# The order of SP's loads between the end of the attention and the output projection of a hybrid encoder block

## The chip, the cores and the metric

One core of a Trainium2 chip runs the whole block in one launch. The metric is device time in microseconds (us). Three runs of the kernel before gave a median of 1238.97 us (1238.19 to 1239.67). One more execution was profiled; all rows below come from it.

## What is computed

The reference, cut to the parts that this case touches. All arrays are float32; the sequence is 1024 tokens plus 16 meta tokens, the model width is 1024, and the MLP is 4096 wide.

```python
def hybrid_mixer(u, ...):
    z = jnp.einsum('bld,dn->bln', u, w_in)
    a, q, k, v, r, lr, ga, gb = jnp.split(z, IN_SPLITS, axis=-1)
    ...
    y_a = jnp.einsum('blc,cd->bld', p, w_pool_out)
    ...
    o = gla_chunked(q, k, v, log_a)
    o = rmsnorm(o, gla_norm...) * jax.nn.silu(r)...
    y_b = jnp.einsum('blc,cd->bld', o.reshape(B, L, GLA_VAL), w_gla_out)
    m = jax.nn.sigmoid(ga) * y_a + jax.nn.sigmoid(gb) * y_b
    return jnp.einsum('bld,de->ble', m, w_out)

def reference(x, ...):
    ...
    h = h + hybrid_mixer(rmsnorm(h, norm_mix[l]), ...)
    h = h + squared_relu_mlp(rmsnorm(h, norm_ffn[l]), w_ff1[l], w_ff2[l])
    return rmsnorm(h, norm_final)[:, N_META:]
```

## The kernel before

Every float32 product is made of three passes over rounded operands: each operand is split into a high part (`hi`, written by ACT with a copy that rounds) and a low part (`lo`, the remainder, written by DVE or POOL with a subtraction), and `mm3` (lines 246 to 248) issues high by high, high by low and low by high into one PSUM bank. A weight therefore takes three steps before PE may use it: SP's DMA brings it into a raw tile, ACT makes the high part, DVE (or POOL) makes the low part.

The work is a list of steps that runs once in the order of the program. PE keeps that order. Two regions have a hand-made order on other engines too: `in_order(True)` in `early_gates` starts a stretch in which ACT and DVE are kept in program order, and `wo1_open` ends it. Everywhere else, and on SP and POOL in the whole kernel, a scheduler sets the order when the program is built. Each engine, SP's queue included, works through its list in order: an instruction that waits holds back all that stand behind it.

The stretch of this case, in the order of the program:

- **The last attention unit** closes: `across` (from line 1216) normalizes the result and writes the high and low parts of `yg` (lines 1280 and 1281). PE fills its waits with blocks of the product with `w_gla_out`.
- **The gates.** `yb_block(n, h)` multiplies `yg` by a 256-column block of `w_gla_out`, two output tiles of 128 by 512 for each block, for the token half h. Each of the eight output tiles of a half is called a gate here, G0 to G7 in half 0 and H0 to H7 in half 1. A gate takes 12 matmuls, two loads (`gl` from `gb_dram`, line 1008, and `ml` from `ma_dram`, line 1009), two DVE operations (line 1060 takes the product out of PSUM and multiplies it by `gl`, line 1061 adds `ml`), an ACT operation (`th`, line 1064) and a POOL operation (`tl`, line 1065). The tiles for the loads rotate over three places in each half, so the loads of a gate wait for the DVE and POOL operations of the gate three back.
- **The blocks' weights** go through the ring `W1` (class `Ring`, lines 58 to 80): raw load at line 101, high part at line 77, low part at line 78. Half 1 uses the blocks 2, 3, 0, 1: the blocks 2 and 3 are kept from half 0, and blocks 0 (gates H4, H5) and 1 (gates H6, H7) are loaded again.
- **The output weights.** `load_wo(ch, kk)` loads 256 rows of one column half of `w_out` (512 KB) into a raw tile (line 101), makes the high part on ACT (line 1345) and the low part on DVE (line 1346). The four pieces of the first column half are called kk0 to kk3. They share the two raw tiles, and a third one (`raw3`), with the ring's loads: `raw.lend(S["raw3"])` in `merge_open`.
- **x again.** `x_again(t)` (line 1337) loads the t-th tile of 128 rows of x (512 KB) into `acc[:, t]`, since the residual is added there.
- **The output projection.** `out_tile(t, ch)` multiplies rows tile t of the merged gates by column half ch of `w_out`, 24 matmuls, and DVE adds the bank into `acc` (line 1378). The eight tiles of ch 0 run first; tile 0 needs kk0 to kk3 one after the other, 6 matmuls each. After ch 1 the rows are normalized and turned for the MLP.

Four PSUM banks rotate over the gates of half 1 and the tiles of the projection, so a gate or tile needs the bank of the fourth one before it to have been taken out by DVE.

Of the kernel before, what the change touches and what calls it, by code (L numbers as in the profile page):

```python
# [15 lines left out]
P = 128  # L16
D = 1024
# [3 lines left out]
HALF = 512  # L21
# [15 lines left out]
class Stack:  # L37


    def __init__(self, tc, side):  # L40
        self.tc, self.side, self.pools = tc, side, []
# [17 lines left out]
class Ring:  # L59


    def __init__(self, nc, raw, hi, lo, depth):
        self.nc, self.raw, self.hi, self.lo, self.depth = nc, raw, hi, lo, depth
        self.queue, self.loaded, self.done, self.kept = [], 0, 0, 0
        self.views = {}
        self.eng = nc.vector

    def top_up(self):
        while self.loaded < min(self.done + self.depth, len(self.queue)):
            ap = self.queue[self.loaded]  # L70
            s = self.loaded % self.depth
            n = 1
            for k in ap.shape[1:]:
                n *= k
            raw = self.raw.load(ap, n)
            hi, lo = self.hi[:, s, :n], self.lo[:, s, :n]
            self.nc.scalar.activation(hi, raw, ACT.Copy)
            self.eng.tensor_tensor(lo, raw, hi.bitcast(F32), ALU.subtract)
            self.views[self.loaded] = (hi, lo)
            self.loaded += 1  # L80
# [25 lines left out]
def kernel(  # L106
# [3 lines left out]
    nc = tc.nc  # L110
# [3 lines left out]
    w_gate_up, b_gate, gla_norm, w_gla_out, w_out = w_gate_up[0], b_gate[0], gla_norm[0], w_gla_out[0], w_out[0]  # L114
# [65 lines left out]
    raw = Raw(nc, [left.push(f"raw{i}", [P, D], F32) for i in range(2)])  # L180
    W1 = Ring(nc, raw, left.push("w1h", [P, 2, D], F32R), left.push("w1l", [P, 2, D], F32R), 2)
# [9 lines left out]
    def f32(ap):  # L191
        return ap.bitcast(F32)
# [4 lines left out]
    def bcast(v):  # L197
        return v[None, :].broadcast_to([P, D])
# [599 lines left out]
    one = []  # L798
# [122 lines left out]
    def rows4(w, j):  # L921
        return w[:, j * 256 : (j + 1) * 256].rearrange("(k p) c -> p k c", p=P)
# [79 lines left out]
    def yb_load(n, h):  # L1002

        if n >= 8 or (n, h) in staged:
            return
        d = 2 * YB[h][n // 2] + n % 2
        gl, ml = staged[n, h] = (nxt("t2"), nxt("o2")) if h else (nxt("t1"), nxt("o"))
        nc.sync.dma_start(gl, gb_dram[d, h])
        nc.sync.dma_start(ml, ma_dram[d, h])

    def in_order(on):


        if on:
            S["order"] = tc.manual_schedule(engines={mybir.EngineType.Activation, mybir.EngineType.DVE})
            S["order"].__enter__()
        else:
            S.pop("order").__exit__(None, None, None)

    def early_gates():  # L1020

        in_order(True)
        left.pop_to(S["left_n"])
        for key in ("t2", "o2"):
            S[key] = right.push(key, [P, 3, HALF], F32)
            S["n" + key], S["d" + key] = 0, 3
        S["raw3"] = right.push("raw3", [P, D], F32)
        for n in range(3):
            yb_load(n, 1)

# [294 lines left out]
    def merge_open():  # L1325
        W1.eng = dve
        banks(keep=1, x=2, ms=4)
        rota["mm"] = ("mm", "mm", "x", "x")
        left.pop_to(base)
        S["wo"] = [left.push("wo0", [P, 2, KT, HALF], F32R)]  # L1330
        S["left_acc"] = left.mark()
        S["acc"] = left.push("acc", [P, 8, D], F32)
        raw.lend(S["raw3"])
        nc.sync.dma_start(gB, bcast(norm_ffn))

    def x_again(t):
        nc.sync.dma_start(S["acc"][:, t], x[t * P : (t + 1) * P, :])

    def load_wo(ch, kk):
        def fn():  # L1340
            wo = S["wo"][ch][:, :, 2 * kk : 2 * kk + 2]
            c = slice(ch * HALF, (ch + 1) * HALF)
            r = raw.load(w_out[kk * 256 : (kk + 1) * 256, c].rearrange("(k p) c -> p k c", p=P), D)
            r = r.rearrange("p (k c) -> p k c", k=2)
            act.activation(wo[:, 0], r, ACT.Copy)
            dve.tensor_tensor(wo[:, 1], r, f32(wo[:, 0]), ALU.subtract)

        return fn

    step(one, merge_open)  # L1350
    def wo1_open():
        in_order(False)
        raw.back()
        right.pop_to(0)
        buffer("u2", 2, D)
        S["u2p"] = right.push("u2p", [P, 2, HALF], F32)
        S["rawx0"] = right.push("rawx0", [P, D], F32)
        raw.lend(S["rawx0"])
        S["right_ff"] = right.mark()
        S["wo"].append(right.push("wo1", [P, 2, KT, HALF], F32R))  # L1360
# [54 lines left out]
            dve.tensor_tensor(fl, a, f32(fh), ALU.subtract)  # L1415

    for n, j in enumerate(YB[1]):
        if n < 2:
            step(one, yb_block(n, 1))
        else:  # L1420
            step(one, yb_block(n, 1), W1, [rows4(w_gla_out, j)])
        if n:
            step(one, load_wo(0, n - 1))
    step(one, load_wo(0, 3))
    step(one, wo1_open)
    for t in range(8):
# [12 lines left out]
    for t in ORDER[:6]:  # L1439
        step(one, out_tile(t, 1))  # L1440
# [258 lines left out]
```

## Time and profile before

| what | value |
|---|---|
| median of 3 runs | 1238.97 us (1238.19 to 1239.67) |
| the profiled execution | 1239.98 us |
| its span, first to last instruction | 1238.2 us |
| PE busy in the span | 1207.4 us (98%) |
| DVE, ACT, POOL busy | 852.3, 618.3, 66.3 us |
| mean granted clock of PE | 0.995 |
| PE busy from 500 to 600 us | 93.90 of 100 us, clock 0.97 |

The profiled execution's time is 1.78 us above its span; that is the time around the first and the last instruction. Changes inside the span are added to or taken from the median. In a timeline row the columns are start in us, duration in us, engine, line, operation, the tile written and the tile read, and the count; in brackets stands the idle time ahead of it on its engine and what ended that.

### The profile page before, as it was taken

To read this page: it belongs to the slowest core of one execution; us is meant where nothing else is said; L and a number is where in the kernel's file an instruction comes from. 1 tells how busy PE (TensorE), PEld (TensorE's weight loads), DVE (VectorE), ACT (ScalarE), POOL (GpSimd) and SP (SyncE) were. 2 spreads that over 40 slices of the span, in tenths; PEclk is the share of its full clock that TensorE was granted. 3 is DMA by queue.
4 is the path that set the end of the run, shared out by engine and by line. 5 is a ranking of instruction groups with operands and counts; after the bars stand their busy time and mean duration, and the time that the engine had idled before them with its cause. 6 is when DMAs were issued, how large, how long until landed. Compare 5 with 4: busy or idle time off the path is not lost.

```text
span 1238.2 us, 18288 instructions
## 1 busy us (share of the span) xinstructions
PE 1207.4 (98%) x6816; PEld 1006.6 (81%) x6816; DVE 852.3 (69%) x1388; ACT 618.3 (50%) x1099; POOL 66.3 (5%) x74
## 2 busy tenths in 40 slices
PE   7999999999999999899999999999999999999997
PEld 6978888888897778688878888888888888888886
DVE  5896676564456686633897776766775877887686
ACT  6677667322446664412664554545554444444554
POOL 2100000001101115400000000000000000000000
PEclk9999999999999999999999999999999999999999
DMA  8033326247102237741144444444559983333532
GB/s 250 2 96 117 111 85 186 61 139 235 35 19 78 69 120 247 264 127 51 70 137 152 164 155 141 158 149 162 162 198 322 342 268 102 94 97 100 162 97 90
DMA packets 142680, 173.84 MB, mean 140 GB/s; under 512 B 10968, under 2 KB 82416, under 8 KB 142592
## 3 DMA queue, kind: packets, MB, share of 16 engines
q1 hardware_dynamic: 142592, 172.68, 43.7%
q8 instruction: 53, 0.87, 0.3%
q14 instruction: 35, 0.29, 0.1%
HBM read 119.17 MB, written 53.48 MB: 139 GB/s over the span
## 4 chain that ended last, share of the span: by engine, by line
PE 87%; DVE 7%; ACT 3%; issue 1%; DMA 1%; SPq 0%; DVEq 0%; ACTq 0%
PE b_mm L246 10%; PE b_mm L247 10%; PE b_mm L248 10%; PE b_ms L248 9%; PE b_ms L246 9%; PE b_ms L247 9%; PE b_x L247 8%; PE b_x L246 8%; PE b_x L248 8%; PE b_sc L1147 1%; PE b_ms L550 1%; PE b_mx L246 1%; PE b_m L1249 1%; PE b_mx L248 1%; PE b_mx L247 1%
## 5 line engine op out<-in xcount | busy, mean ns | idle before, releaser
L246 PE MATMUL b_mm<-th,w1h 128*128 128x512 f32 (+1 forms) x312 | 117.7, 377 | 0.6 <-ACT th L1406 0.6
L247 PE MATMUL b_mm<-tl,w1h 128*128 128x512 f32 (+1 forms) x312 | 116.2, 372 | 0.6 <-DVE tl L1407 0.6
L248 PE MATMUL b_mm<-th,w1l 128*128 128x512 f32 (+1 forms) x312 | 116.0, 372 | 0.0
L246 PE MATMUL b_x<-th,w1h 128*128 128x512 f32 (+1 forms) x240 | 90.8, 378 | 0.0
L247 PE MATMUL b_x<-tl,w1h 128*128 128x512 f32 (+1 forms) x240 | 90.7, 378 | 0.0
L248 PE MATMUL b_x<-th,w1l 128*128 128x512 f32 (+1 forms) x240 | 90.4, 377 | 0.0
L264 ACT ACTIVATE w1h<-raw 128x512 fp32r<-128x512 f32 x96 | 59.5, 620 | 34.7 <-PE b_x L247 14.1
L265 DVE TENSOR_TENSOR w1l<-raw,w1h 128x512 fp32r<-128x512 f32 x96 | 65.7, 685 | 10.9 <-ACT w1h L264 10.9
L264 ACT ACTIVATE w1h<-fs 128x512 fp32r<-128x512 f32 x72 | 45.4, 630 | 46.2 <-PE b_ms L247 31.8
L246 PEld LDWEIGHTS b_mm<-th,w1h 128*128 128x128 f32 x312 | 58.6, 188 | 12.0 <-ACT th L1406 1.0
L247 PEld LDWEIGHTS b_mm<-tl,w1h 128*128 128x128 f32 x312 | 58.7, 188 | 10.6 <-DVE tl L1407 0.9
L248 PEld LDWEIGHTS b_mm<-th,w1l 128*128 128x128 f32 x312 | 58.7, 188 | 10.3
L264 ACT ACTIVATE w1h<-bt 128x512 fp32r<-128x512 f32 x44 | 27.8, 632 | 67.9 <-issue 63.6
L265 DVE TENSOR_TENSOR w1l<-fs,w1h 128x512 fp32r<-128x512 f32 x72 | 49.3, 686 | 14.7 <-ACT w1h L264 14.6
L1556 DVE TENSOR_TENSOR bt<-w,w 128x512 f32<-128x512 f32 x80 | 54.7, 684 | 1.1 <-DMA w<-in_w_ff_dram 1.1
L248 PEld LDWEIGHTS b_x<-th,w1l 128*128 128x128 f32 x240 | 45.2, 188 | 8.4
L246 PEld LDWEIGHTS b_x<-th,w1h 128*128 128x128 f32 x240 | 45.1, 188 | 8.4
L247 PEld LDWEIGHTS b_x<-tl,w1h 128*128 128x128 f32 x240 | 45.1, 188 | 8.2
L264 ACT ACTIVATE fxh<-bt 128x512 fp32r<-128x512 f32 x36 | 22.8, 632 | 54.9 <-issue 49.2
L247 PE MATMUL b_ms<-wo,w1h 128*128 128x512 f32 x128 | 49.8, 389 | 0.0
L248 PE MATMUL b_ms<-wo,w1l 128*128 128x512 f32 x128 | 49.8, 389 | 0.0
L246 PE MATMUL b_ms<-wo,w1h 128*128 128x512 f32 x128 | 49.8, 389 | 0.0
(446 smaller groups left out, 3373.9 us busy)
## 6 DMA issues: line engine op xcount, KB each, us to landing
hf_dram<-h SPq DMA_DIRECT2D x112, 256.0 KB, 2.1
raw<-hf_dram SPq DMA_DIRECT2D x112, 256.0 KB, 2.7
w<-in_w_ff_dram SPq DMA_DIRECT2D x64, 256.0 KB, 4.7
raw<-in_w_in_dram SPq DMA_DIRECT2D x24, 512.0 KB, 4.8
raw<-in_w_ff_dram SPq DMA_DIRECT2D x16, 512.0 KB, 4.1
rawx<-in_w_ff_dram SPq DMA_DIRECT2D x16, 512.0 KB, 4.2
xs<-in_x_dram SPq DMA_DIRECT2D x8, 512.0 KB, 4.6
rawx<-in_w_in_dram SPq DMA_DIRECT2D x8, 512.0 KB, 4.6
```

The source lines that it names most:

```text
L246: pe.matmul(ps, ah, bh, start=first and i == 0, stop=False, skip_group_check=more)
L247: pe.matmul(ps, ah, bl, start=False, stop=False, skip_group_check=more)
L248: pe.matmul(ps, al, bh, start=False, stop=last and i == n - 1, skip_group_check=more)
L264: act.activation(hi, a, ACT.Copy)
L265: dve.tensor_tensor(lo, a, f32(hi), ALU.subtract)
L550: pe.transpose(b[j][:, i], u[:, (4 * j + i) * P : (4 * j + i + 1) * P], ident)
L1147: pe.matmul(b[to, e, j], kk[r, s], qq[r, s], start=True, stop=True, tile_position=(e * CH, u * CH))
L1249: pe.matmul(o[part(u), e, j], scc[part(u), e, j], v[part(u), j, e], start=j == 0, stop=False, tile_position=(u * CH, u * CH), skip_group_c ...
L1556: dve.tensor_tensor(bt, w, S["w2"][q[3:]][:, i], ALU.add if q[2] == "+" else ALU.subtract)
```

## The change

- `Ring` gets a `fetch` that issues raw loads ahead of the conversions, and `top_up` uses what was fetched.
- `merge_open` closes the ordered stretch of ACT and DVE and opens it again, and from there to `first_blocks` SP's loads stand in program order too (`in_order("loads", ...)`).
- The third raw tile is no longer lent to the ring. It takes kk0, issued in `early_gates` ahead of the gates of half 1. kk1, kk2 and kk3 are loaded into `acc[:, 5]`, `acc[:, 6]` and `acc[:, 7]`, which hold nothing yet at that time.
- `load_wo(0, n)` moves ahead of the block n of half 1, where it stood behind the block n + 1.
- The x loads, and the load of the norm's weights (`gB`), move behind the last gate's loads; x then runs two tiles ahead of the projection.
- No arithmetic is added or removed.

```diff
+    def fetch(self, count):
+
+        for ap in self.queue[self.loaded + len(self.fetched) :][:count]:
             n = 1
             for k in ap.shape[1:]:
                 n *= k
-            raw = self.raw.load(ap, n)
+            self.fetched.append((self.raw.load(ap, n), n))
+
+    def top_up(self):
+        while self.loaded < min(self.done + self.depth, len(self.queue)):
+            s = self.loaded % self.depth
+            if not self.fetched:
+                self.fetch(1)
+            raw, n = self.fetched.pop(0)
...
     def early_gates():
...
         S["raw3"] = right.push("raw3", [P, D], F32)
+        fetch_wo(0, 0, S["raw3"])
         for n in range(3):
             yb_load(n, 1)
...
         S["acc"] = left.push("acc", [P, 8, D], F32)
-        raw.lend(S["raw3"])
+        any_order("order")
+        in_order("loads", mybir.EngineType.SP)
+        in_order("order", mybir.EngineType.Activation, mybir.EngineType.DVE)
+        W1.fetch(2)
+        fetch_wo(0, 1, S["acc"][:, 5])
+
+    def load_gB():
         nc.sync.dma_start(gB, bcast(norm_ffn))
...
     for n, j in enumerate(YB[1]):
+        step(one, load_wo(0, n))
         if n < 2:
             step(one, yb_block(n, 1))
         else:
             step(one, yb_block(n, 1), W1, [rows4(w_gla_out, j)])
-        if n:
-            step(one, load_wo(0, n - 1))
-    step(one, load_wo(0, 3))
+        if n < 2:
+            step(one, lambda kk=n + 2: fetch_wo(0, kk, S["acc"][:, 4 + kk]))
+    step(one, load_gB)
     step(one, wo1_open)
+    step(one, lambda: x_again(0))
+    step(one, lambda: x_again(1))
     for t in range(8):
-        step(one, lambda t=t: x_again(t))
+        if t < 6:
+            step(one, lambda t=t: x_again(t + 2))
         step(one, out_tile(t, 0))
         if 1 < t < 6:
             step(one, load_wo(1, t - 2))
...
     def first_blocks():
+        any_order("loads")
```

PE's and POOL's instructions keep their order. What moves on the other engines, as the built programs have it, at the three places that matter:

**Place 1, the gate G3 in the attention's close.** ACT, from the gates G1 and G2 (`th_131` is half 0's high part, `w1h` the ring's) to the first operations of the last normalization, before:

```order
L1064 ACTIVATE th_131<-t_2709 128x512 x2
L77 ACTIVATE w1h<-raw_115 128x1024
L1064 ACTIVATE th_131<-t_2709 128x512
L1268 ACTIVATE mix<-b_m_4639 128x1024
L210 ACTIVATE small<-small 128x8
L212 ACTIVATE small<-small 128x8
```

and of the change:

```order
L1071 ACTIVATE th_131<-t_2709 128x512 x2
L1369 ACTIVATE wo_4805<-raw_4539 128x1024
L83 ACTIVATE w1h<-raw_115 128x1024
L1071 ACTIVATE th_131<-t_2709 128x512
L1275 ACTIVATE mix<-b_m_4640 128x1024
L216 ACTIVATE small<-small 128x8
L218 ACTIVATE small<-small 128x8
```

DVE at the same place, from gate G2's sum to the reduction that starts the normalization, before:

```order
L1061 TENSOR_TENSOR t_2709<-t_2709,o 128x512
L1254 COPY small<-b_m_4639 128x2
L1060 TENSOR_TENSOR t_2709<-b_mm,t_2709 128x512
L1061 TENSOR_TENSOR t_2709<-t_2709,o 128x512
L1271 TENSOR_REDUCE small<-mix 128x8
L211 TENSOR_SCALAR small<-small 128x8
```

and of the change:

```order
L1068 TENSOR_TENSOR t_2709<-t_2709,o 128x512
L1261 COPY small<-b_m_4640 128x2
L1067 TENSOR_TENSOR t_2709<-b_mm,t_2709 128x512
L1370 TENSOR_TENSOR wo_4805<-raw_4539,wo_4805 128x1024
L1068 TENSOR_TENSOR t_2709<-t_2709,o 128x512
L1278 TENSOR_REDUCE small<-mix 128x8
L217 TENSOR_SCALAR small<-small 128x8
```

The high part of kk0 stands ahead of the ring's weight and of G3's `th` on ACT, and its low part stands between the two operations of G3 on DVE.

**Place 2, the gates of half 1.** ACT, from the last gates of half 0 over the ring's two weights to the last gates (`th_139` is half 1's), before:

```order
L1064 ACTIVATE th_139<-t_4531 128x512
L77 ACTIVATE w1h<-raw_119 128x1024
L1064 ACTIVATE th_139<-t_4531 128x512 x2
L77 ACTIVATE w1h<-raw_4539 128x1024
L1064 ACTIVATE th_139<-t_4531 128x512
L1345 ACTIVATE wo_4804<-raw_115 128x1024
L1064 ACTIVATE th_139<-t_4531 128x512 x2
L1345 ACTIVATE wo_4804<-raw_119 128x1024
L1064 ACTIVATE th_139<-t_4531 128x512 x2
L1345 ACTIVATE wo_4804<-raw_4539 128x1024
L1345 ACTIVATE wo_4804<-raw_115 128x1024
```

and of the change:

```order
L1071 ACTIVATE th_139<-t_4531 128x512
L83 ACTIVATE w1h<-raw_119 128x1024
L1071 ACTIVATE th_139<-t_4531 128x512
L1369 ACTIVATE wo_4805<-acc 128x1024
L1071 ACTIVATE th_139<-t_4531 128x512
L83 ACTIVATE w1h<-raw_115 128x1024
L1071 ACTIVATE th_139<-t_4531 128x512
L1369 ACTIVATE wo_4805<-acc 128x1024
L1071 ACTIVATE th_139<-t_4531 128x512 x2
L1369 ACTIVATE wo_4805<-acc 128x1024
L1071 ACTIVATE th_139<-t_4531 128x512 x2
```

Before, kk0, kk1 and the pair kk2 and kk3 followed H3, H5 and H7; now kk1 stands between H1 and H2, ahead of the ring's second weight, kk2 behind H3 and kk3 behind H5. The low parts on DVE moved in the same way: kk1's stands behind H1's sum and ahead of H2, kk3's behind H5 and ahead of H6.

**Place 3, SP's queue over half 1** (`t_4531` and `o_4535` are the gates' loads of half 1), before, from G7's load on:

```order
L1008 DMA t_2709<-gb_dram 128x512
L1337 DMA acc<-in_x_dram 128x1024
L1008 DMA t_4531<-gb_dram 128x512
L1009 DMA o_4535<-ma_dram 128x512
L1337 DMA acc<-in_x_dram 128x1024
L101 DMA raw_119<-in_w_out_dram 128x2x512
L1008 DMA t_4531<-gb_dram 128x512
L1009 DMA o_4535<-ma_dram 128x512
L1008 DMA t_4531<-gb_dram 128x512
L1009 DMA o_4535<-ma_dram 128x512
L101 DMA raw_4539<-in_w_out_dram 128x2x512
L1009 DMA o_4535<-ma_dram 128x512
```

and of the change, from kk1 to the last gate's load:

```order
L1361 DMA acc<-in_w_out_dram 128x2x512
L1014 DMA t_4531<-gb_dram 128x512
L1015 DMA o_4535<-ma_dram 128x512
L1361 DMA acc<-in_w_out_dram 128x2x512
L1014 DMA t_4531<-gb_dram 128x512
L1015 DMA o_4535<-ma_dram 128x512
L1014 DMA t_4531<-gb_dram 128x512
L1015 DMA o_4535<-ma_dram 128x512
L1361 DMA acc<-in_w_out_dram 128x2x512
L1014 DMA t_4531<-gb_dram 128x512
L1015 DMA o_4535<-ma_dram 128x512
L1014 DMA t_4531<-gb_dram 128x512
```

kk1 took the place of the first x load, the x loads left the stretch, and all four pieces of the first column half are issued ahead of the loads of H6.

More of the change, by code (lines that the diff above doesn't have):

```diff
@@ L63, in __init__ @@
         self.nc, self.raw, self.hi, self.lo, self.depth = nc, raw, hi, lo, depth
-        self.queue, self.loaded, self.done, self.kept = [], 0, 0, 0
+        self.queue, self.loaded, self.done, self.kept, self.fetched = [], 0, 0, 0, []
         self.views = {}
         self.eng = nc.vector
[L68 to L71, printed above, removed]
+    def fetch(self, count):
+        for ap in self.queue[self.loaded + len(self.fetched) :][:count]:
             n = 1
@@ L1009, in yb_load, with in_order, any_order @@
         nc.sync.dma_start(ml, ma_dram[d, h])
[L1011 to L1018, printed above, removed]
+    def in_order(key, *engines):
+        S[key] = tc.manual_schedule(engines=set(engines))
+        S[key].__enter__()
+    def any_order(key):
+        S.pop(key).__exit__(None, None, None)
     def early_gates():
-        in_order(True)
+        in_order("order", mybir.EngineType.Activation, mybir.EngineType.DVE)
         left.pop_to(S["left_n"])
@@ L1332, in merge_open @@
         S["acc"] = left.push("acc", [P, 8, D], F32)
-        raw.lend(S["raw3"])
+        any_order("order")
+        in_order("loads", mybir.EngineType.SP)
+        in_order("order", mybir.EngineType.Activation, mybir.EngineType.DVE)
+        W1.fetch(2)
+        fetch_wo(0, 1, S["acc"][:, 5])
+    def load_gB():
         nc.sync.dma_start(gB, bcast(norm_ffn))
@@ L1337, in x_again, with fetch_wo @@
         nc.sync.dma_start(S["acc"][:, t], x[t * P : (t + 1) * P, :])
+    fetched = {}
+    def fetch_wo(ch, kk, at=None):
+        c, rows = slice(ch * HALF, (ch + 1) * HALF), w_out[kk * 256 : (kk + 1) * 256]
+        ap = rows[:, c].rearrange("(k p) c -> p k c", p=P)
+        if at is None:
+            at = raw.load(ap, D)
+        else:
+            nc.sync.dma_start(at.rearrange("p (k c) -> p k c", k=2), ap)
+        fetched[ch, kk] = at.rearrange("p (k c) -> p k c", k=2)
     def load_wo(ch, kk):
         def fn():
[L1341 to L1344, printed above, removed]
+            if (ch, kk) not in fetched:
+                fetch_wo(ch, kk)
+            wo, r = S["wo"][ch][:, :, 2 * kk : 2 * kk + 2], fetched.pop((ch, kk))
             act.activation(wo[:, 0], r, ACT.Copy)
@@ L1351, in wo1_open @@
     def wo1_open():
-        in_order(False)
+        any_order("order")
         raw.back()
```

## The prediction

> **What bounds the kernel now.** The page has PE busy for 98% of the span, so only PE's idle time can be won. The list of PE's waits shows most of it at one place (waiter, line, releaser: us in all, times, longest):
>
> ```profile
> PE b_mm L246 <- ACT wo L1345: 4.1, 1, 4.1
> PE b_mm L247 <- DVE wo L1346: 2.0, 2, 1.4
> ```
>
> Both are tile 0 of the output projection, waiting for the high and low parts of w_out. PE's timeline, from gate H6 to the second tile:
>
> ```profile
> 509.54 0.39 PE L246 MATMUL b_x<-yg,w1h 128*128 128x512 f32 x1
> ...
> 514.98 0.39 PE L246 MATMUL b_mm<-wo,th 128*128 128x512 f32 x1
> ...
> 518.29 0.50 PE L247 MATMUL b_mm<-wo,th 128*128 128x512 f32 x1 [1.36 <-DVE wo L1346]
> ...
> 523.78 0.80 PE L246 MATMUL b_mm<-wo,th 128*128 128x512 f32 x1 [4.05 <-ACT wo L1345]
> ...
> 529.44 0.39 PE L246 MATMUL b_x<-wo,th 128*128 128x512 f32 x1
> ```
>
> H6 and H7, 24 matmuls, took 514.98 - 509.54 = 5.44 us (0.227 each). Tile 0, also 24, took 529.44 - 514.98 = 14.46. So 9.02 us are lost, of which 6.1 are waits; the rest is a halved clock after them (windows: start and end, length, busy us of PE, PEld, DVE, ACT and POOL, PEclk, DMA share, GB/s):
>
> ```profile
> 521.00:522.00 1.00, 0.00 (x0) 0.00 (x0) 0.97 (x2) 0.00 (x0) 0.57 (x1) 0.90 0.78 215
> 522.00:528.00 6.00, 3.53 (x8) 2.47 (x9) 4.36 (x5) 4.64 (x5) 1.27 (x1) 0.50 0.85 320
> 528.00:529.00 1.00, 1.00 (x5) 0.83 (x4) 0.62 (x1) 0.00 (x0) 0.00 (x0) 0.69 0.96 324
> ```
>
> Why the weights came late, on ACT, DVE and SP:
>
> ```profile
> 522.15 0.63 ACT L1064 ACTIVATE th<-t 128x512 fp32r<-128x512 f32 x1 [1.92 <-DVE t L1061]
> 522.69 1.99 ACT L1345 ACTIVATE wo<-raw 128x1024 fp32r<-128x1024 f32 x2
> 520.50 0.69 DVE L1060 TENSOR_TENSOR t<-b_mm,t 128x512 f32<-128x512 f32 x1 [0.94 <-DMA t<-gb_dram]
> 512.13 0.38 SPq L101 DMA_DIRECT2D raw<-in_w_out_dram  x1
> 515.94 0.33 SPq L1008 DMA_DIRECT2D t<-gb_dram  x1
> ```
>
> kk2 and kk3 (the pair at 522.69) stand on ACT behind the last gate H7, whose load left SP only at 515.94. Tile 0 needs half 0 alone, so H7 need not have held it.
>
> **The change, part by part.** *Removed: the 9.02 us.* kk2 and kk3 now stand ahead of H7, with their loads ahead of H6's. If no new wait arises, the gain is 9.0, its upper end. The four copies and four subtractions are paid for all the same, now inside the gates.
>
> *kk0 inside G3.* The rows of G2 and G3 on ACT and DVE, the end of the attention's chain, a low part of w_out beside POOL, and the two PE instructions that need the chain:
>
> ```profile
> 479.15 0.63 ACT L1064 ACTIVATE th<-t 128x512 fp32r<-128x512 f32 x1 [1.92 <-DVE t L1061]
> 480.36 0.69 DVE L1060 TENSOR_TENSOR t<-b_mm,t 128x512 f32<-128x512 f32 x1 [0.73 <-PE b_mm L248]
> 481.08 0.69 DVE L1061 TENSOR_TENSOR t<-t,o 128x512 f32<-128x512 f32 x1
> 481.81 0.63 ACT L1064 ACTIVATE th<-t 128x512 fp32r<-128x512 f32 x1 [0.58 <-DVE t L1061]
> 482.35 1.01 ACT L1268 ACTIVATE mix<-b_m 128x1024 f32<-128x1024 f32 x1
> 486.30 1.23 DVE L1273 TENSOR_TENSOR mix<-b_m,small 128x1024 f32<-128x1024 f32 x1
> 492.44 1.23 DVE L1281 TENSOR_TENSOR yg<-mix,yg 128x1024 fp32r<-128x1024 f32 x1 [1.13 <-ACT yg L1280]
> 510.64 1.47 DVE L1346 TENSOR_TENSOR wo<-raw,wo 128x1024 fp32r<-128x1024 f32 x1 [1.65 <-ACT wo L1345]
> 488.92 1.03 PE L1277 MATMUL b_m<-ident,mix 128*128 128x128 f32 x8
> 494.81 0.39 PE L247 MATMUL b_mm<-yg,w1h 128*128 128x512 f32 x1
> ```
>
> ACT's copy fits behind G2's th (479.7 to 480.75). DVE's low part goes in after 480.36 and takes about 1.45 less the 0.1 by which neighbours overlap, so G3's sum moves from 481.08 to 482.4, and with it G3's th and L1268, which starts the last normalization: all of it is 1.35 later. The transposes at 488.92 need the end of L1273: 487.53 + 1.35 = 488.9, just in time. The matmul at 494.81 needs yg's low part: 493.67 + 1.35 = 495.0. **Cost 0.2** (0 to 0.7, with the longest such low part at 1.83). Gates G4 to H1 inherit about 1.3 us; PE has the banks it needs by then.
>
> The ring's reload for G6 and G7 moves on SP behind G2's and G3's loads to where the r load stood, which landed in 4.5 us:
>
> ```profile
> 474.44 0.39 SPq L1266 DMA_DIRECT2D mix<-r_dram  x1
> mix<-r_dram SPq DMA_DIRECT2D x1, 512.0 KB, 4.5
> ```
>
> So it lands near 479, before ACT takes it at about 480.65: nothing.
>
> *kk1 between H1 and H2.* Its tile in acc lies where the attention's tiles were, so its load waits, as the first x load did, for G7's POOL operation, the second of these three:
>
> ```profile
> 495.74 4.69 POOL L1065 TENSOR_TENSOR tl<-t,th 128x512 fp32r<-128x512 f32 x3 [3.16 <-ACT th L1064]
> 499.21 0.33 SPq L1337 DMA_DIRECT2D acc<-in_x_dram  x1
> acc<-in_x_dram SPq DMA_DIRECT2D x1, 512.0 KB, 3.7
> raw<-in_w_out_dram SPq DMA_DIRECT2D x1, 512.0 KB, 4.5
> ```
>
> Issued 1.3 later, at 500.5, it lands between 504.2 and 505.0. What is queued behind it:
>
> ```profile
> 502.88 0.63 ACT L1064 ACTIVATE th<-t 128x512 fp32r<-128x512 f32 x1 [3.13 <-DVE t L1061]
> 504.74 1.05 ACT L77 ACTIVATE w1h<-raw 128x1024 fp32r<-128x1024 f32 x1
> 505.82 1.84 DVE L78 TENSOR_TENSOR w1l<-raw,w1h 128x1024 fp32r<-128x1024 f32 x1 [1.65 <-ACT w1h L77]
> ```
>
> These are H1's th and the ring's last weight, for H6 and H7. Before, that weight was done at 507.66; H6's third matmul, the first to read the low part, came 0.45 after 509.54, at 510.0: 2.3 us spare. Now H1's th starts at 504.2, kk1's copy runs from 504.7 to 505.8, its low part to 507.2, H2's two DVE operations (0.7 each) to 508.6, H2's th for 0.54 (its start to its neighbour's), the weight's copy to 510.2, its low part to 512.05. That is 4.4 later: 4.4 - 2.3 - 0.2 (PE already late) = **1.85 us of new stall in H6**. Bounds: 0.7 (low parts of 1.2, and no inheritance beyond 0.7) to 3.2 (kk1 landing 1.3 later).
>
> *kk2 and kk3.* From 512.05 on DVE: H3 to 513.4; th and kk2's copy on ACT to 515.0; its low part to 516.5; H4 and H5 to 519.15; th and kk3's copy to 520.8; its low part to 522.25. Tile 0 starts at 514.98 + 0.2 + 1.85 = 517.05, or 517.1 with H4's bank. It reads kk3's low part 19 matmuls later, at 521.4: **0.85** (0 to 1.3), plus 0.05 for the bank.
>
> *x, gB and the second half of w_out* now leave SP from about 520.5. Tile 0's bank is wanted again by tile 4, at 518 + 4 x 5.44 = 539.7, and x's first tile lands by 530 even at twice the longest landing quoted here. Thirteen loads of 512 KB at the 320 GB/s of the window above take 21 us, so all are in by 543; the second half is read at 518 + 8 x 5.44 = 561.5. Nothing, with 9 us of cover at the least; without it each us late would count in full.
>
> **Sum:** -9.0 + 0.2 + 1.85 + 0.05 + 0.85 = -6.05, say -6.0. The profiled execution would take 1239.98 - 6.0 = 1234.0 (span 1232.2); the median shown lies 1.0 lower, so **1233.0**.
>
> **Rivals.** *The new stall halves the clock too.* For: above, the clock fell at 522, only some 2 us into the long wait, when a short one had gone before. Against:
>
> ```profile
> 405.00:406.00 1.00, 0.30 (x6) 0.33 (x8) 0.93 (x4) 0.00 (x0) 0.00 (x0) 1.00 0.57 92
> PE b_m L1249 <- DVE S L1242: 1.6, 1, 1.6
> ```
>
> There a wait of 1.6, ending in this stretch, left it at 1.00. H6's 1.85 lies between. A clock at 0.50 for the 6.6 us seen from 521.8 to 528.4, now full of work, loses 3.3; tile 0 then comes later, so kk3's 0.85 vanishes: 2.4 net, **1235.4**. The Trainium skill, "TensorE: Matmul & The Clock Gate", Part 1 (the HAM clock gate), says that the clock halves after at least one idle window of about 3.4 us. By that rule H6's wait would not trip it and the sum stays at 1233.0; the trace's earlier fall agrees only in part.
>
> *The waits are mostly covered.* With low parts of 1.2 us H6's stall is near 0.7 and kk3's nothing; 7.5 to 8.5 us are won: **1231.0**. For: without POOL beside it a low part can be quick. Against: POOL's th-to-tl work runs in every gate.
>
> *kk1's load holds everything (slower).* ACT keeps kk1's copy ahead of H2 and the ring's last weight, so each us that it lands after 504.7 is a us of PE in H6, and the clock falls besides. The gain of 6.0 less 2.4 is used up at 3.6 us late, and the kernel is over 0.2% slower from 6.1 late, a landing of 10.3 us. At 6.5 late: 1233.0 + 2.4 + 6.5 = **1241.9**. For: it waits for POOL, the slowest engine here, and a gate's loads follow on its heels. Against: the two landings above.
>
> That the change doesn't do what it says is ruled out by the built order: all four pieces stand ahead of H6.
>
> **Chances.** Forecast (won 4.5 to 7.5): 0.50. Mostly covered (over 7.5): 0.17. Clock (2.5 to 4.5): 0.19. kk1 moderately late, within 2.5 us of before: 0.08. kk1 very late: 0.06. A measurement of this kernel can tell about 0.2%, 2.5 us, from no change: faster 0.86, same 0.08, slower 0.06. Range 1230.0 (all 9 won) to 1237.3 (1.7 won); it leaves out the late half of the fourth case, the fifth and a little below.
>
> **What would show it.** PE's waits at tile 0 for wo's high part are gone, and the clock stays 1.00 from 520 to 530; a wait of 1 to 3 us at H6 for L84 (the ring's low part), one under 1.3 at tile 0 for wo's low part, and 0.0 to 0.7 in H0 for yg. kk1 issued near 500.5, landed by 505. H6's wait above 3, or a clock of 0.5 there, makes it wrong towards slower; no wait at H6 at all means that I sized the chain on ACT and DVE too long.

## The result, and the profile after

| kernel | runs | median, us | lowest to highest | ratio to before, 95% interval |
|---|---|---|---|---|
| before | 7 | 1239.54 | 1238.19 to 1240.51 | |
| the change | 7 | 1235.07 | 1233.88 to 1237.71 | 0.9968 (0.9956 to 0.9979) |

The change is 4.5 us faster by the medians, 4.0 by the ratio. The forecast was 1233.0 in a range of 1230.0 to 1237.3. The profiled execution of the change took 1236.75 us with a span of 1235.0, 1.7 us above the median of the seven. PE is busy for 98% of the span as before, with a granted clock of 0.997 (before 0.995).

PE's list of waits (waiter, line, releaser: us in all, times, longest) no longer has wo's high part. Six of its waits matter here:

```profile
PE b_m L1284 <- DVE mix L1280: 1.5, 1, 1.5
PE b_mm L252 <- ACT th L1430: 1.2, 1, 1.2
...
PE b_mm L253 <- DVE wo L1370: 0.9, 1, 0.9
...
PE b_x L254 <- DVE w1l L84: 0.8, 1, 0.8
PE b_mm L253 <- DVE tl L1431: 0.6, 1, 0.6
...
PE b_x L252 <- ACT w1h L83: 0.5, 1, 0.5
```

PE's timeline shows where they lie. The lines have moved: mm3 is at 252 to 254, the transposes of the close at 1284.

```profile
489.23 1.09 PE L1284 MATMUL b_m<-ident,mix 128*128 128x128 f32 x8 [1.52 <-DVE mix L1280]
...
510.86 0.50 PE L252 MATMUL b_x<-yg,w1h 128*128 128x512 f32 x1 [0.46 <-ACT w1h L83]
...
512.35 0.50 PE L254 MATMUL b_x<-yg,w1l 128*128 128x512 f32 x1 [0.76 <-DVE w1l L84]
...
517.47 0.42 PE L252 MATMUL b_mm<-wo,th 128*128 128x512 f32 x1
...
522.93 0.50 PE L253 MATMUL b_mm<-wo,th 128*128 128x512 f32 x1 [0.94 <-DVE wo L1370]
...
524.20 0.39 PE L252 MATMUL b_x<-wo,th 128*128 128x512 f32 x1
...
626.19 0.49 PE L252 MATMUL b_mm<-th,w1h 128*128 128x512 f32 x1 [1.22 <-ACT th L1430]
...
627.33 0.50 PE L253 MATMUL b_mm<-tl,w1h 128*128 128x512 f32 x1 [0.64 <-DVE tl L1431]
```

Tile 0 now takes 524.20 - 517.47 = 6.73 us; it took 14.46. Four waits are left between the close and tile 0, and two lie 100 us further on, in the feed-forward layers. The windows (length, busy us of PE, PEld, DVE, ACT and POOL, PEclk, DMA share, GB/s) show that the clock is whole where it was halved before, and halved at a place where it was whole:

```profile
522.00:528.00 6.00, 5.07 (x22) 4.22 (x23) 3.46 (x5) 1.26 (x2) 2.99 (x2) 1.00 0.94 311
...
624.00:627.00 3.00, 1.47 (x6) 0.66 (x4) 3.00 (x6) 2.07 (x5) 0.00 (x0) 1.00 0.00 0
...
628.00:631.00 3.00, 3.00 (x9) 2.31 (x8) 3.00 (x6) 1.14 (x2) 0.00 (x0) 0.50 0.00 0
```

PE runs the same instructions in the same order in every kernel of this study, so a matmul can be found in each trace and its start set against that of before. The table does this at seven matmuls, at 473, 495.3, 515.0, 529.4, 627.2, 640.1 and 1230.2 us of the trace before. Each column is what the stretch between two of them took more (+) or less (-) than before, in us. The last is the sum behind 473. At 473 the executions already differ from that of before, from 1.5 us ahead of it to 0.2 behind, also among those that have the change's instructions up to there. Most of this is there at 20 us already. The change has no part in it, and it is left out.

| profiled execution | close (473 to 495) | gates H (to 515) | tile 0 (to 529) | to 627 | 627 to 640 | to the end | sum |
|---|---|---|---|---|---|---|---|
| the change | +2.06 | +1.80 | -7.73 | 0.00 | +2.17 | -0.15 | -1.85 |
| again | +2.05 | +1.74 | -7.72 | -0.03 | +2.30 | -0.14 | -1.80 |
| low0_later | -0.01 | +1.63 | -7.78 | 0.00 | +0.02 | +0.17 | -5.97 |
| kk1_behind | +0.05 | +0.05 | -7.79 | -0.02 | +0.20 | -0.11 | -7.62 |
| by_hand | 0.00 | 0.00 | -9.02 | -0.02 | +0.10 | -0.12 | -9.06 |
| low0_pool | +0.79 | +1.57 | -7.73 | +0.02 | +0.09 | +0.20 | -5.06 |
| store_later | +0.06 | +1.69 | -7.73 | -0.02 | +2.10 | -0.12 | -4.02 |
| loads_alone | -0.01 | 0.00 | -0.65 | 0.00 | +0.20 | -0.09 | -0.55 |
| places_alone | -0.01 | +5.30 | -9.02 | +0.04 | -0.02 | -0.11 | -3.82 |
| by_hand_store | +0.14 | +0.04 | -9.02 | -0.01 | -0.38 | -0.14 | -9.37 |
| sum_behind | +2.05 | +1.54 | -7.70 | -0.01 | +0.06 | -0.14 | -4.20 |
| by_hand_sum | -0.01 | 0.00 | -9.02 | 0.00 | +0.04 | -0.15 | -9.14 |

So two losses of some 2 us each were not in the forecast: one at the close and one at 627 to 640. The experiments ask what makes them, and whether each forecast term stands by itself.

### The profile page after: what moved, and what is told of

It is laid out like the page before. It is cut to its first block, busy times and chain, and to the rows that moved or that the text cites. A ratio compares the mean times of both kernels' runs of the same rounds, so it can differ in the third digit from the quotient of the medians.

```text
span 1235.0 us, 18287 instructions
## 1 busy us (share of the span) xinstructions
PE 1204.8 (98%) x6816; PEld 1003.1 (81%) x6816; DVE 852.0 (69%) x1388; ACT 618.3 (50%) x1099; POOL 66.8 (5%) x74
## 4 chain that ended last, share of the span: by engine, by line
PE 87%; DVE 7%; ACT 3%; issue 1%; DMA 1%; POOL 0%; SPq 0%; DVEq 0%; ACTq 0%
PE b_mm L252 10%; PE b_mm L253 10%; PE b_mm L254 10%; PE b_ms L252 9%; PE b_ms L254 9%; PE b_ms L253 9%; PE b_x L253 8%; PE b_x L252 8%; PE b_x L254 8%; PE b_sc L1154 1%; PE b_ms L556 1%; PE b_mx L252 1%; PE b_m L1256 1%; PE b_mx L254 1%; PE b_mx L253 1%
```

## The experiments

**The change again.** Nothing is edited; it ran beside the three that follow.

> The changed kernel once more, beside those that it is compared with. It shows which of its losses come back in a second execution. All theories: the add of G3 on DVE (L1068) takes 2.9 us again and PE waits about 1.5 us for mix at the close; H6 waits about 0.46 and 0.76 us for the ring's weight; tile 0 waits about 0.9 us for wo's low part. Open is the stretch at 618 to 632: if the late landing of the rawx load (1.11 us of wait on DVE) is only how this one execution went, the TensorE clock stays at 1.00 there and the span is some 2 us shorter; if it belongs to the change, the wait of 1.2 us for th L1430 and the fall to 0.50 at 628 come back.

Median 1235.19 us over 9 runs (1232.65 to 1236.97), ratio 0.9967 (0.9958 to 0.9977). All losses came back in the profiled execution, the fall of the clock at 628 too. Over the 16 runs of the change the times spread by 5.1 us.

**The close: is DVE's add held beside POOL?** The rows of the change at G3, DVE and then POOL, show what happened:

```profile
478.99 0.69 DVE L1067 TENSOR_TENSOR t<-b_mm,t 128x512 f32<-128x512 f32 x1 [0.73 <-PE b_mm L254]
479.59 1.22 DVE L1370 TENSOR_TENSOR wo<-raw,wo 128x1024 fp32r<-128x1024 f32 x1
480.73 2.90 DVE L1068 TENSOR_TENSOR t<-t,o 128x512 f32<-128x512 f32 x1
...
480.17 2.90 POOL L84 TENSOR_TENSOR w1l<-raw,w1h 128x1024 fp32r<-128x1024 f32 x1 [1.28 <-ACT w1h L83]
```

kk0's low part was quicker than I had taken it, 1.22 us. But G3's add behind it, 0.69 before, took 2.90. It ended at 483.63, 0.56 behind the end of POOL's operation. The first experiment moves only kk0's low part on DVE to behind H0's work:

```diff
+                if h and e and not n:
+                    low0.pop()()
                 if e and not wbs:
...
-            dve.tensor_tensor(wo[:, 1], r, f32(wo[:, 0]), ALU.subtract)
+            low = lambda: dve.tensor_tensor(wo[:, 1], r, f32(wo[:, 0]), ALU.subtract)
+            if ch or kk:
+                low()
+            else:
+                low0.append(low)
```

> Only kk0's low part (DVE L1370) moves, from between the two DVE operations of gate G3 to behind those of gate H0; its copy on ACT stays, and so POOL's low part of the ring's weight starts when it did. Theory A (the add of G3 was held beside POOL because kk0's low part pushed it behind the start of POOL's operation): the add starts near 479.7, takes 0.69 us, PE does not wait for mix or for yg, and the kernel is 1.9 us faster than the change, bounds 1.2 to 2.2, near 1233.2 median. The waits of H6 stay as they are. Theory B (the add is slow for another reason, such as the copies on ACT or the new loads): it takes 2.9 us again, ends near 482.6 at the latest 483.6, and less than 0.5 us is won.

Median 1233.51 us (1232.99 to 1233.77), ratio 0.9953 (0.9941 to 0.9966): 1.7 us faster than the change beside it, and the runs spread by 0.8 us only. DVE and POOL in this execution:

```profile
480.59 0.69 DVE L1072 TENSOR_TENSOR t<-t,o 128x512 f32<-128x512 f32 x1
...
481.05 2.49 POOL L84 TENSOR_TENSOR w1l<-raw,w1h 128x1024 fp32r<-128x1024 f32 x1 [1.28 <-ACT w1h L83]
```

The add starts ahead of POOL and takes 0.69; the loss at the close is gone (-0.01 in the table). This leaves open whether POOL holds the add or DVE's own low part does. So in the next one kk0's low part goes to POOL, and DVE has nothing between G3's two operations:

```diff
-            dve.tensor_tensor(wo[:, 1], r, f32(wo[:, 0]), ALU.subtract)
+            (dve if ch or kk else pool).tensor_tensor(wo[:, 1], r, f32(wo[:, 0]), ALU.subtract)
```

> kk0's low part goes to POOL, ahead of POOL's low part of the ring's weight; everything else is as in the change, and DVE has G3's two operations next to one another. One look at the trace, for the hold. Theory A (a DVE operation with both operands in SBUF that comes up while POOL works waits until POOL's operation ends): POOL's kk0 operation runs from about 479.2 to 481.7, G3's add on DVE comes up at 479.7 and ends 0.55 after it, near 482.2, 2.5 us long; if POOL's next operation holds it too, near 484.8. Theory B (it is the low part on DVE itself that makes the add long): the add takes 0.69 and ends at 480.4.

One run, 1233.80 us. DVE and POOL:

```profile
479.72 2.44 DVE L1068 TENSOR_TENSOR t<-t,o 128x512 f32<-128x512 f32 x1
...
479.23 2.38 POOL L1370 TENSOR_TENSOR wo<-raw,wo 128x1024 fp32r<-128x1024 f32 x1 [0.33 <-ACT wo L1369]
481.57 2.85 POOL L84 TENSOR_TENSOR w1l<-raw,w1h 128x1024 fp32r<-128x1024 f32 x1
```

The add took 2.44 us with no other work on DVE, and ended at 482.16, 0.55 behind the end of POOL's first operation. Theory A holds in place and size, and B has fallen.

**H6: is it kk1 ahead of the ring's last weight?** kk1 goes behind that weight, next to kk2:

```diff
     for n, j in enumerate(YB[1]):
-        step(one, load_wo(0, n))
+        for kk in ((0,), (), (1, 2), (3,))[n]:
+            step(one, load_wo(0, kk))
```

> kk1's copy and low part move from between H1 and H2 to behind the ring's last weight, with kk2's beside them; kk0 and kk3 stay. Theory A (H6 waits because kk1 waits for its DMA on ACT and DVE ahead of H2 and of that weight): the waits of 0.46 and 0.76 us at H6 go, 1.8 us are won there; kk3's low part comes as late as before, and tile 0 reaches it 1.8 us earlier, so its wait of 0.94 us grows by 0.2 to 0.5; net 1.5 us faster than the change, 0.8 to 1.8. Theory B (the ring's weight is late because of its own load or of its slot): the waits at H6 stay, 0.

Median 1233.52 us (1231.50 to 1235.88), ratio 0.9961 (0.9948 to 0.9975), 1.7 us faster than the change. The gates lose +0.05 instead of +1.8, so theory A holds. Tile 0's wait for kk3 did not grow (0.91 us), against the expectation: kk3's work came earlier with the gates. By chance this execution shows more of the close. The instructions there are those of the change, yet nothing was lost. ACT, DVE and POOL:

```profile
480.12 1.06 ACT L83 ACTIVATE w1h<-raw 128x1024 fp32r<-128x1024 f32 x1 [0.45 <-DMA raw<-in_w_gla_out_dram]
...
481.25 0.68 DVE L1068 TENSOR_TENSOR t<-t,o 128x512 f32<-128x512 f32 x1
...
481.26 2.94 POOL L84 TENSOR_TENSOR w1l<-raw,w1h 128x1024 fp32r<-128x1024 f32 x1 [1.85 <-PE b_m L1266]
```

The ring's reload landed 0.45 us late for ACT, and POOL started 0.01 us behind the add. Now the add takes 0.68, and POOL 2.94, where it took 2.49 in low0_later. So the loss depends on which of the two starts first. Three of the executions with this order (the change, again, and sum_behind below) lost 2.05 or 2.06 at the close, two (this one and store_later below) 0.05 and 0.06.

**All three losses at once.** The high and the low parts are emitted apart: kk0's low part behind H0's work, the ring's last weight ahead of kk1, copies ahead of a gate's operations and low parts behind them, kk2 and kk3 both loaded right behind H1:

```diff
+    PRE_HI, PRE_LO = {0: (0,)}, {1: (0,)}
+    MID_HI, MID_LO = {3: (1, 2)}, {3: (1,)}
+    POST_HI, POST_LO = {4: (3,)}, {4: (2,), 5: (3,)}
...
+                g = 2 * n + e if h else None
+                split_wo(hi=PRE_HI.get(g, ()), lo=PRE_LO.get(g, ()))
                 if e and not wbs:
                     W1.done, W1.kept = W1.done + 1, W1.kept - 1
                     W1.top_up()
...
+                split_wo(hi=MID_HI.get(g, ()), lo=MID_LO.get(g, ()))
                 dve.tensor_tensor(gl, b, gl, ALU.mult)
...
+                split_wo(hi=POST_HI.get(g, ()), lo=POST_LO.get(g, ()))
...
     for n, j in enumerate(YB[1]):
-        step(one, load_wo(0, n))
...
-        if n < 2:
-            step(one, lambda kk=n + 2: fetch_wo(0, kk, S["acc"][:, 4 + kk]))
+        if n == 0:
+            step(one, lambda: fetch_wo(0, 2, S["acc"][:, 6]))
+            step(one, lambda: fetch_wo(0, 3, S["acc"][:, 7]))
```

> All three at once, with the high and low parts placed apart: kk0's low part behind H0, the ring's last weight ahead of kk1, both kk2 and kk3 loaded right behind kk1, copies ahead of gates and low parts between gates. If the losses are the three that I name (1.9 at the close, 1.8 at H6, 1.1 at tile 0) they add up: 4.8 us faster than the change, bounds 3.3 to 5.2, near 1230.3 median. If they hide behind one another (DVE as the bound from H0 to tile 0), only the largest goes and it wins 2 to 2.5 us, the rest coming back as waits at tile 0 or for a bank. A rival: what is won here comes back at 618 to 632, where DVE is the bound, and less than half of it reaches the end.

Median 1230.29 us (1229.61 to 1232.77), ratio 0.9932 (0.9919 to 0.9944): 4.9 us faster than the change, as the sum of the three losses had it. From the last gates to tile 1 PE has no gap, in the timeline and in a window:

```profile
513.68 0.39 PE L252 MATMUL b_mm<-wo,th 128*128 128x512 f32 x1
...
519.12 0.39 PE L252 MATMUL b_x<-wo,th 128*128 128x512 f32 x1
```

```profile
500.00:520.00 20.00, 20.00 (x90) 16.56 (x89) 17.35 (x19) 8.34 (x11) 9.97 (x7) 1.00 0.68 230
```

Tile 0 takes 5.44 us here. The losses did not hide behind one another, though DVE was busy for 17.35 of the 20 us.

**One part alone.** First the change's loads, with the conversions where they stood before:

```diff
     for n, j in enumerate(YB[1]):
-        step(one, load_wo(0, n))
...
+        if n:
+            step(one, load_wo(0, n - 1))
+    step(one, load_wo(0, 3))
```

> The change with its loads in the new order, but the copies and low parts of w_out's first half back where they stood before: kk0 behind H3, kk1 behind H5, kk2 and kk3 behind H7. Theory A (the place of the conversions on ACT and DVE is what counts): the losses at the close and at H6 go, H7's loads come on time, but kk2's copy still follows H7's th, which ends near 521.5; PE gets kk2 about 1.2 us earlier than before and still waits 3 us or so, and the clock halves again; 1 to 2.4 us faster than before, near 1237.9 median, 2.8 slower than the change. Theory B (the late loads were what held tile 0): as fast as the change or faster, 1233 to 1235.

Median 1238.83 us over 11 runs (1237.73 to 1239.59), ratio 0.9994 (0.9985 to 1.0003). That is less than I expected. PE still waits for kk2's copy behind the last gate, and the clock halves as before:

```profile
521.49 0.80 PE L252 MATMUL b_mm<-wo,th 128*128 128x512 f32 x1 [2.84 <-ACT wo L1369]
```

Then the kernel before, with the four steps `load_wo(0, n)` in the change's places. In this kernel a step holds the load of its piece too, so the loads of w_out move with the conversions. x, the three raw tiles and SP's free order stay:

```diff
     for n, j in enumerate(YB[1]):
+        step(one, load_wo(0, n))
...
-        if n:
-            step(one, load_wo(0, n - 1))
-    step(one, load_wo(0, 3))
```

> The kernel before with its loads as they were (x first, w_out through the three slots of raw, SP's order free) and only the conversions moved: kk0 ahead of H0's work, kk1, kk2 and kk3 ahead of H2's, H4's and H6's. Theory A (the place of the conversions on ACT and DVE is what counts, the loads follow): the 9.0 us at tile 0 go but for the chain's waits at H6 and for kk3, and the close loses nothing, since kk0 is not pulled up into it; 4 to 7 us faster than before, near 1234.5 median. Theory B (without SP's order the loads of x and the three slots hold kk2 and kk3 up): 0 to 2.5 us faster, with PE waiting for kk2's or kk3's high part at tile 0.

Median 1234.92 us (1234.34 to 1235.35), ratio 0.9962 (0.9950 to 0.9975): as fast as the change. Tile 0 won all of its 9.02 us, though x was loaded first. But kk0's conversion now stood in the gates of half 1, H6 lost more, and there the clock was halved:

```profile
510.81 0.50 PE L246 MATMUL b_x<-yg,w1h 128*128 128x512 f32 x1 [2.10 <-ACT w1h L77]
...
512.30 0.57 PE L248 MATMUL b_x<-yg,w1l 128*128 128x512 f32 x1 [0.75 <-DVE w1l L78]
```

```profile
513.00:516.00 3.00, 3.00 (x8) 2.32 (x8) 1.36 (x2) 1.58 (x2) 1.28 (x1) 0.50 0.89 231
```

So the gain needs the new places on ACT and DVE, and tile 0 needs neither x's new place nor a fixed order on SP. The order of SP's loads, after which the change is named, wins half a us by itself in the trace, which the runs cannot tell from nothing. The places are not parted from w_out's own loads, though: kk1's load left SP at 483.18 us here (501.84 before), kk2's at 503.40 (507.69 before). And the equal medians hide a difference. Up to the end of tile 0, places_alone won 3.73 us in the table, and low0_later, which has the change's loads without its loss at the close, 6.16. So beside the new places the rest of the change is worth some 2 us there, in one execution of each.

**627 to 640: what halves the clock?** Before PE's two waits there, DVE waits for a 512 KB load of w_ff. DVE's row, and SP's row of the load:

```profile
617.52 0.69 DVE L321 TENSOR_TENSOR fs<-rawx 128x512 f32<-128x512 f32 x1 [1.11 <-DMA rawx<-in_w_ff_dram]
...
612.39 0.38 SPq L298 DMA_DIRECT2D rawx<-in_w_ff_dram  x1
```

From there DVE has no gap until PE's waits are over, so PE waits for DVE. Before, the same wait was 0.49 us (at 622.14). In all eleven executions with such a wait on DVE, from 0.16 to 1.22 us, PE's first wait is longer than it by 0.08 to 0.11 us. The first kernel moves away a store that leaves SP 0.8 us behind the load. In this kernel the last tile of h is stored after the turn of that tile has overwritten it, so this tile's output is not that of the reference.

```diff
-                nc.sync.dma_start(h_dram[t], S["acc"][:, t])
+                n < 7 and nc.sync.dma_start(h_dram[t], S["acc"][:, t])
...
-        ff_room()
+        nc.sync.dma_start(h_dram[7], S["acc"][:, 7]), ff_room()
```

> The change with one store moved: that of the last h tile to h_dram, which now leaves SP 0.8 us behind the rawx load and shares the DMA engines with it, leaves after gB's load, ahead of the release of acc. Theory A (the store slows the rawx load, whose landing DVE waits for, and the wait at 626 then halves the clock): the load lands 0.5 to 1.1 us earlier, DVE's wait falls from 1.1 to 0.0 to 0.6, PE's wait for th L1430 from 1.2 to 0.1 to 0.7, the clock stays at 1.00 from 625 to 635; 2.2 us won in the profiled execution (1.5 to 2.7), and some 1 to 2 us in the median of all, since the fall need not come in each. Theory B (the load takes as long by itself): no change within 0.5 us, the clock falls again.

Median 1235.07 us (1234.56 to 1236.06), ratio 0.9965 (0.9953 to 0.9978). The load took 5.0 us from issue to landing with no store beside it (5.1 in the change), DVE waited 1.01, PE 1.09 and 0.64, and the clock fell again. Theory A has fallen here. The same edit on the version by hand:

> The version placed by hand, with the last h tile's store behind gB's load too. There PE still waited 0.67 and 0.63 us at 620 with the clock at 1.00. Theory A: the first of these falls by 0.3 to 0.6, 1229.9 median, and the spread of the runs shrinks, since no run loses the clock there. Theory B (the store is not what delays the load): the same as the version by hand, 1230.3 within 0.5.

Median 1229.14 us (1228.96 to 1230.89), ratio 0.9919 (0.9907 to 0.9932); this kernel's output is not that of the reference either. There the load took 4.1 us (4.6 in by_hand), DVE waited 0.16 and PE's first wait was 0.27. With the store behind it the load took 4.5 to 5.2 us in eleven executions, without it 5.0 and 4.1. So the store does not decide the landing by itself; whether it has a part is not shown by two executions, and I did not find what else delays the load.

The next one leaves the load as it is and takes DVE's wait from the front of the queue. The sum fs<-rawx stands behind the first part of the turn of tile 6:

```diff
...
+        if after:
+            after()
...
+    def second_sum():
+        a21, a22 = (ff_quarters.w[1, 1][:, k : k + 4] for k in (0, 4))
+        dve.tensor_tensor(quad(S["fs"][:, 1]), a21, a22, ALU.add)
...
-            if n in (1, 3):
-                turn_tile(ORDER[6 + n // 2])
+            if n == 1:
+                in_order("turn", mybir.EngineType.DVE)
+                turn_tile(ORDER[6], after=second_sum)
+                any_order("turn")
+            if n == 3:
+                turn_tile(ORDER[7])
```

> The change with one DVE operation moved, 100 us behind it: the sum fs<-rawx, which waits for the rawx load at the front of DVE's queue, now stands behind the first four pieces of work of the turn of tile 6; a subtraction (fs<-fs,raw) comes up in its old place. Theory A (at 618 to 632 DVE is the bound, its wait for the late rawx load makes PE wait for th, and that wait together with the next one halves the clock): DVE does not wait for rawx any more; of the 1.0 to 1.2 us, 0.6 go to the subtraction; PE's wait for th falls from 1.1 to 1.3 to 0.5 to 0.8, as in the executions that kept the clock, and the clock stays at 1.00 in 625 to 635; 1.5 to 2.3 us faster than the change in the profiled execution, some 1 us in the median, 1234. Theory B (the fall comes from elsewhere): the clock falls again and nothing is won.

Median 1235.24 us (1232.73 to 1235.95), ratio 0.9962 (0.9950 to 0.9975): the median does not show the us that I expected. The profiled execution lost 2.05 at the close, and was 1.6 us later than the other two of the change when it came there; neither has to do with the edit. In the trace the clock stayed whole, in PE's timeline and in the window:

```profile
627.29 0.49 PE L252 MATMUL b_mm<-th,w1h 128*128 128x512 f32 x1 [1.01 <-ACT th L1432]
...
628.10 0.50 PE L253 MATMUL b_mm<-tl,w1h 128*128 128x512 f32 x1 [0.31 <-DVE tl L1433]
```

```profile
629.00:632.00 3.00, 3.00 (x15) 2.46 (x14) 3.00 (x6) 1.54 (x3) 0.00 (x0) 1.00 0.00 0
```

The waits sum to 1.32 instead of 1.86, and 627 to 640 loses 0.06 instead of 2.17. The first wait stayed at 1.01, above the 0.5 to 0.8 expected; the second fell to 0.31. This fits theory A, but does not show it by itself. The load landed in 4.8 us here, and in the change DVE was ready for it 4.0 us behind its issue. So in its old place this sum of DVE would have waited about 0.8 us (an estimate), and kk1_behind kept the clock with 0.73. The last kernel has this edit on the version by hand:

> The version placed by hand and the moved sum together. Theory A: by hand PE lost 0.67 and 0.63 there without losing the clock; the sum's move wins 0 to 0.5 in such an execution and keeps the slowest ones from losing the clock: 1229.9 median, none above 1231.5. Theory B: 1230.3, with one run in five near 1232.5 as before.

Median 1229.99 us (1229.56 to 1230.29), ratio 0.9923 (0.9910 to 0.9937). PE's waits there sum to 1.28, against 1.30 by hand, so nothing is won in the profiled execution; the five runs spread by 0.7 us instead of 3.2, but how the clock went in the others is not shown. This is the fastest kernel of the study that computes the reference, 9.4 us faster than before.

## Why the prediction was right, and where it was not

The forecast of faster held, and the time lies 2.1 us above the forecast, within the range. How near the median came is in part luck. Two losses of some 2 us each, which the forecast did not have, came in some of the profiled executions only. In the one of the change, the stretches behind 473 us won 1.85 us where 6.05 were forecast; the other 1.37 us of its shorter span were won ahead of 473, where the change has no part. The clock rival's 1235.4 is the nearest number to the median, also by luck: its fall of the clock at H6 did not come, and the fall at 628 was in no rival. By its own steps:

- **The removed 9.0 us: right.** by_hand and places_alone win 9.02 at tile 0.
- **kk0 inside G3, 0.2 us with bounds of 0 to 0.7: wrong.** This is the step that failed: it cost 2.06, or nothing. I moved G3's add by the length of the low part and left its own length at 0.69. What decided was whether the add or POOL's low part of the ring's weight starts first, and no row of the prediction has that POOL operation. Before, the add at 481.08 was only 0.23 ahead of it (the last row below). The trace of before also had a warning, an add that took 1.41 and ended 0.55 behind a POOL operation:

```profile
477.70 1.41 DVE L1061 TENSOR_TENSOR t<-t,o 128x512 f32<-128x512 f32 x1 [0.55 <-DMA o<-ma_dram]
...
477.30 1.26 POOL L1065 TENSOR_TENSOR tl<-t,th 128x512 fp32r<-128x512 f32 x1 [2.43 <-ACT th L1064]
...
481.31 2.72 POOL L78 TENSOR_TENSOR w1l<-raw,w1h 128x1024 fp32r<-128x1024 f32 x1 [0.16 <-ACT w1h L77]
```

  Counted from the start of G3's product on DVE (480.36 before, 478.99 in the change), the add started 0.72 behind it before and 1.74 in the change, POOL's operation 0.95 and 1.18. So POOL did not start earlier; kk0's low part alone put the add behind it. The step "The ring's reload ... nothing" has no part in the loss. Where the reload landed late for ACT, by 0.45 and 0.49 (kk1_behind, store_later), POOL started just behind the add, and nothing was lost.

  The Trainium skill, "SBUF — State Buffer", section "Who interferes with whom", says that a DVE instruction with two SBUF inputs contends with a GpSimd instruction that reads SBUF, and that issue order decides which of the two blocks. The rows agree in both directions: 2.90 and 2.44 for the add behind POOL's start, 0.68 for the add and 2.94 for POOL when the add was first.
- **kk1 ahead of the ring's last weight, 1.85: right**, 1.80 and 1.74, and gone with kk1 behind the weight. The waits were two, 0.46 for the high part and 0.76 for the low part, where one of 1 to 3 us for the low part was forecast; the rest went in the matmuls around them.
- **kk3's low part, 0.85 (0 to 1.3), and 0.05 for the bank: too small.** Tile 0 took 6.73 against 5.44, so 1.29 were lost, at the upper bound; 0.94 is the wait itself, the rest the matmuls around it.
- **x, gB and the second half of w_out, nothing: right.** No wait of PE in the list names them.
- **What is won reaches the end: wrong.** No term stood for the feed-forward layers, and 2.17 were given back there. PE's wait follows a wait on DVE that stood in the trace before with 0.49 and that the change does not touch. That the two waits led to the fall of the clock is borne out by all thirteen traces together (last section), not by sum_behind alone; why the load lands late in some executions is open.
- **The rival that the new stall halves the clock: not at H6** with its waits of 0.46 and 0.76. places_alone shows the mechanism at that very place, with 2.10 and 0.75.

With neither of the two losses the forecast sum of -6.05 is met: low0_later has -5.97 and a median of 1233.51. The change itself loses 2 us at the close in some executions and 2 us at 627 in some. That its 16 runs spread over just such levels (1232.65 to 1237.71) is argued from three profiled executions of this order, not shown run by run.

## What to carry to other kernels

An operation that is put into a gap on one engine has two prices: its own length, and which instruction of a neighbour engine now starts first; look in the trace for operations whose length changes beside another engine before taking a length as fixed. Where a tuned order moves work earlier, price the places on the engines that convert before the order of the loads, and place each piece behind the work that PE needs next. A kernel whose runs spread by 5 us where its neighbour's spread by 0.8 may have a race in it that is worth finding.

## What the runs showed of the hardware

- **DVE and POOL exclude each other over a whole instruction** when DVE's add has both operands in SBUF, and a lead of 10 or 40 ns is enough: with POOL 0.01 or 0.04 us behind (kk1_behind, store_later), the add took 0.68; with POOL 0.56 ahead, 2.90. An operation with a PSUM operand was not held. In the change, in the midst of three POOL operations, the product with the bank kept its 0.68 and the add behind it took 1.08:

```profile
497.89 0.68 DVE L1067 TENSOR_TENSOR t<-b_mm,t 128x512 f32<-128x512 f32 x1
498.61 1.08 DVE L1068 TENSOR_TENSOR t<-t,o 128x512 f32<-128x512 f32 x1
...
497.39 4.71 POOL L1072 TENSOR_TENSOR tl<-t,th 128x512 fp32r<-128x512 f32 x3 [3.15 <-ACT th L1071]
```

- **The clock went by PE's busy time in fixed stretches of 3.41 us, and short waits add up in one.** Within each trace the changes of the granted clock lie whole multiples of 3.413 us apart. Before, it fell at 78.06 and 521.79 us and came back at 81.48 and 528.62, so the fall at tile 0 lasted 6.83 us (the prediction read 6.6). From 20 us to PE's last matmul the thirteen traces hold 4579 such stretches. Each of the eleven in which PE was busy for 1.68 us or less was followed by one at 0.50, and no other was; the next two had 1.69 and 1.71 (again and by_hand, near 75 us). The change, and then kk1_behind, at the two waits of the feed-forward layers:

```profile
624.58:627.99 3.41, 1.55 (x6) 0.76 (x5) 3.41 (x7) 1.91 (x5) 0.00 (x0) 1.00 0.00 0
627.99:631.40 3.41, 3.41 (x10) 2.63 (x9) 3.41 (x6) 1.15 (x2) 0.00 (x0) 0.50 0.00 0
...
619.33:622.74 3.41, 2.60 (x12) 1.77 (x10) 3.41 (x7) 2.52 (x6) 0.00 (x0) 1.00 0.02 7
622.74:626.15 3.41, 2.78 (x12) 2.10 (x12) 3.41 (x7) 2.09 (x4) 0.00 (x0) 1.00 0.00 0
```

  The change's waits of 1.22 and 0.64 lie in one stretch, those of kk1_behind, 0.81 and 0.63, in two. So it is not the sum of the waits alone that counts, but how much of it falls into one stretch, and where the stretches begin differs between executions. Ahead of the other falls PE was busy for 1.47 and 1.68 us (again and store_later, near 627) and 1.01 (places_alone, H6). Before, it was 1.34 in the stretch that ended at 521.79; the wait of 1.36 us that ended at 518.29 lies ahead of that stretch, so it is not what made the clock fall so early. The Trainium skill, "TensorE: Matmul & The Clock Gate", Part 1 (the HAM clock gate), has the clock halve after an idle window of about 3.4 us. The length agrees with these traces; that the window is idle does not, since PE was busy in every one of the eleven, and the measurements decide.
